# Another order for the weight pairs of a two-layer decoder step: a gate pair behind the pooling pair and one at the end, attention in ten pairs

## Chip, cores and metric

The kernel runs on one core of a Trainium2 chip. The time is the device time of one execution in microseconds; three runs of the kernel before took 1469.11 to 1471.54 us, with a median of 1469.99.

## What is computed

Two layers, each on 1024 prompt positions and 8 sample rows (T = 1032 columns). All columns of `w_in` come from one projection, then three branches are gated, projected and merged:

```python
xa, za, u, v, zb, q, k, vv, zc, gates = split_in(jnp.einsum('bld,de->ble', x, w_in))
ya = pool_mix(xa, 0, pos, pool_w, pool_scale)          # causal window sums of 2, 4, 8, 16, then a small matmul
yb = u * sgu_spatial(layer_norm(v), sgu_w, sgu_b)      # 128-position chunks
yc = banded_window_attention(rope(q), rope(k), vv, attn_sinks)
g = sigmoid(gates.reshape(lead + (3, D_MODEL)) + b_gate)
oa, ob, oc = (ya * silu(za)) @ w_pa, (yb * silu(zb)) @ w_pb, (yc * silu(zc)) @ w_pc
merged = g[..., 0, :] * oa + g[..., 1, :] * ob + g[..., 2, :] * oc
x = layer_norm(ALPHA * x + merged @ w_out, ln_g, ln_b)
```

## The kernel before

Every matrix product with fp32 data is made of three passes with a high and a low half of each operand (`split`, lines 97 and 98: ScalarE rounds to the high half, VectorE subtracts it from the original to get the low half). XH and XL hold the halves of x, transposed, for all 1032 columns.

The columns of `w_in` that don't need attention's rotary step are worked in 18 pairs of 128 columns each, from the weight `wS[l, p]`, p = 0 to 17: 12 gate pairs (p = 0 to 11, branch i = p // 4, columns d and d + 1), the pooling input xa (12), za (13), zb (14), u (15) and two pairs of zc (16, 17). A pair (`pair`, line 863) is a Strassen-like scheme of seven products, in the order 11, 2, 21, 3, 1, 4, 22; a product is 24 matmuls of 128 x 258 (line 862), four PSUM banks (`acc`) are in use, and VectorE's adds (line 878) and a ScalarE copy (line 888) empty a bank before it is used again. The result goes to two tiles `O`, and `use` finishes them: for a gate pair, tanh on ScalarE (line 928) and a store of both tiles to HBM (`gd`, line 930, issued by ScalarE); for za and zb, tanh and a product on VectorE (line 628); for zc, tanh and two products on VectorE for each of 8 pieces (lines 941 and 942), which also multiply the attention result in place. Weight halves come from `prep`: POOL makes sums of the weight quarters (lines 210 to 219), ScalarE and VectorE split them, SyncE loads the raw weights in the order that `order()` lists (line 92).

The tiles u4 to u11 are single buffers that many stages use in turn: gate pairs write u6/u7 or u8/u9 by turns, za goes to u8/u9, the pooling input to u6/u7, its running sums to u4/u5 and u10/u11.

All other work lies beside the pairs as jobs (`Jobs`). A pair calls `pump` 21 times, three times in each product; each call is a tick. In a tick at most one job with matrix work runs, and list 1, attention, runs one for every `pace` ticks (2.8). Attention is 80 jobs with matrix work (scores, transposes, products with v) and as many without (query halves, norms, key halves). Pooling sums (`pool_sums`) are POOL additions in list 3 and VectorE steps in list 2 (widening, line 795; mean, line 805), each some ticks behind the other; `queue_mix` queues six small matmuls (line 821, with line 823 on VectorE behind each). `need(key)` runs whatever is left of a list up to that job at once. Each engine works its queue in the order in which the program issues it.

In the main loop the order is: rotary columns, 12 gate pairs with attention beside them, the pooling pair, za with the pooling sums beside it, zb with the mix, u with the chunk products, zc 0, zc 2, and then `project`. During the last pair, zc 2, hooks split the pooling and chunk branches into halves (`split_y`, four times) and group 0 of the attention branch (`split_c`); groups 1, 3 and 2 are split in the first three steps of `project`.

`project` (line 980) has 24 steps (i, d): branch i into output columns d. A step has two halves of columns, q = 0 into `att` banks and q = 1 into `acc` banks, two banks each of four. Line 1000 multiplies by the gate, which SyncE has loaded back from HBM (`load_gate`, line 973) into u4 to u7; for i > 0 POOL adds it to the merged result (line 1002), and the next gate is loaded into the freed half. The first six steps are (0,0), (1,0), (0,1), (1,1), (2,0), (2,1); a step with i = 0 or 1 has 24 matmuls (line 995), one with i = 2 has 48 and needs the four attention groups.

Of the kernel before, what the change touches and what calls it, by code (L numbers as in the profile page):

```python
# [8 lines left out]
F32 = mybir.dt.float32  # L9
# [12 lines left out]
T = S + NS  # L22
DM = 1024
SEGS = ((0, 384), (384, 384), (768, 264))
ALPHA = 4.0 ** 0.25
EPS = 1e-5


# [73 lines left out]
def trunk_kernel(  # L102
# [44 lines left out]
    def t_u(s, shape, dt=F32, name="u"):  # L147

        return big.tile([128] + shape, dt, tag=s, name=f"{name}{s}")
# [22 lines left out]
    def order():  # L172
        for l in range(L):
            yield from [wA[l, :, k] for k in range(8)]
            yield from [wB[l, j, :, 4 * h:4 * h + 4] for j in range(5) for h in range(2)]
            yield from [wS[l, p, q] for p in range(18) for q in range(4)]
            yield from [wP[l, d, :, h * 512:h * 512 + 512] for h in range(2) for d in range(2)]
            for d in range(2, 8):
                yield from [wP[l, d, :, h * 512:h * 512 + 512] for h in range(2)]
                if d >= 4:  # L180
                    yield wO[l, 0, :, d - 4]
            yield from [wO[l, 0, :, k] for k in range(4, 8)]
            yield from [wO[l, 1, :, k] for k in range(8)]
# [154 lines left out]
    class Layer:  # L338
        def __init__(self, l):
            self.l, self.c, self.jobs = l, LC[l], Jobs()  # L340
            self.s, self.pt, self.res, self.rr, self.row, self.y = [{} for _ in range(6)]
            self.late, self.step, self.out = deque(), 0, []
            self.jobs.pace = 2.8
            self.kT = t_u("u10", [T], F32, "kT")
            self.v = t_u("u11", [NB, 128], F32, "v")
            self.vs = lay.tile([NS, 128], F32, name="vs")
# [4 lines left out]
        def a0_post(self, b, p):  # L351
# [7 lines left out]
            V.bn_aggr(mv[:n], st[:n])  # L359
            rstd_of(mv, n, EPS)  # L360
            vn = vn_dst[:n]
# [267 lines left out]

        def out_of(self, O, c, q, s):  # L630
            o = q * HT + s * 258
            return O[c][:, o:o + 258]

        def pair_xa(self):
            self.xa = O = [t_u(f"u{6 + j}", [T], F32, "xa") for j in range(2)]

# [283 lines left out]
            out(0, 1)  # L920
            pump()

        def gates(self, i, d, extra={}):
            O = [t_u(s, [T], F32, "g") for s in (("u8", "u9") if d % 4 else ("u6", "u7"))]

            def use(c, q, s, p):
                o = O[c][:, q * HT + s * 258:q * HT + s * 258 + 258]
                A.activation(o, p, AF.Tanh, bias=self.c["h"][:, i * 8 + d + c:i * 8 + d + c + 1], scale=0.5)  # L928
                if s and (c, q) in ((1, 0), (0, 1)):
                    A.dma_start(out=gd[i][d + c], in_=O[c])  # L930

            self.pair(use, O, extra)

        def gate_c(self, j, extra={}):
            O = [t_u(s, [T], F32, "z") for s in (("u6", "u7") if j else ("u4", "u5"))]

            def use(c, q, s, p):
                e = slice(q * HT + s * 258, q * HT + s * 258 + 258)
                t, o, y = t_w2()[:, 0:258], O[c][:, e], self.ycr[:, j + c, e]
                A.activation(t, p, AF.Tanh, scale=0.5)  # L940
                V.scalar_tensor_tensor(o, t, 1.0, p, op0=ALU.add, op1=ALU.mult)
                V.scalar_tensor_tensor(y, o, 0.5, y, op0=ALU.mult, op1=ALU.mult)

            self.pair(use, O, extra)

        def split_y(self, j, eng=None):
            h, lo = [t_u(f"x{4 + 2 * j + i}", [T], F32R, "yh") for i in range(2)]
# [32 lines left out]
        def project(self):  # L980
            for x, (i, d) in enumerate(self.steps):
# [5 lines left out]
                for q in range(2):  # L987
# [10 lines left out]
                    for s in range(2):  # L998
                        g = t[:, q * HT + s * 258:q * HT + s * 258 + 258]
# [9 lines left out]
                        self.late.append((self.step + 1, lambda d=d, q=q, m=m[:, e]: self.merged(d, q, m)))  # L1009
                    if (i < 2 and q) or (i == 2 and not q and d >= 3):  # L1010
                        prep()
                if x < 3:
                    self.split_c((1, 3, 2)[x])
                if x == 0:
                    for q in range(2):
                        self.load_gate(0, 1, q)
# [16 lines left out]
        def d_mm(self, b, h, w):  # L1033
# [10 lines left out]
            r = self.row[b][h]  # L1044
            V.scalar_tensor_tensor(r[:n], x[:n, 0:512], 2 * ALPHA, p[:n], op0=ALU.mult, op1=ALU.add)  # L1045
            V.bn_stats(self.rr[b][:n, h * 6:h * 6 + 6], r[:n])  # L1046

        def d_ln(self, b):
# [3 lines left out]
            V.bn_aggr(mv[:n], st[:n])  # L1052
            rstd_of(mv, n, 4 * EPS)
            g, be = c["lng"], c["lnb"]
# [82 lines left out]
    for l in range(L):  # L1137
        y = Layer(l)
        J = y.jobs
# [33 lines left out]
                J.need(("TT", n, k))  # L1173
        y.t1_parts()
        y.queue_sample()
        for i in range(3):
            for d in range(0, 8, 2):
                if (i, d) == (0, 2):
                    J.need("sp")
                y.gates(i, d, {3: lambda: J.need(("T1", 3))} if (i, d) == (0, 0) else {})  # L1180
        J.need(("P", NB - 1, 1))
        y.pair_xa()
        y.ya = y.pair_z(("u8", "u9"))
        y.queue_mix()
        J.need(("pool", 1))
# [3 lines left out]
        y.pair_u()  # L1189
        J.need(("sgu", 1))  # L1190
        y.gate_c(0)
        y.open_gates()
        for i, d in ((0, 0), (1, 0)):
            for q in range(2):
                y.load_gate(i, d, q)
        y.gate_c(2, {2: lambda: y.split_y(0), 21: lambda: y.split_y(1), 3: lambda: y.split_y(2),
                     1: lambda: y.split_y(3), 4: lambda: y.split_c(0)})
        for q in range(2):
            y.load_gate(1, 1, q)
        cur["w0"] = w0 = Slices(WA)  # L1200
# [8 lines left out]
        for i, (b, h) in enumerate(seq):  # L1209
# [9 lines left out]
            if h:  # L1219
                y.d_ln(b)  # L1220
                j = i - 9
# [119 lines left out]
```

## Time and profile before

| | us |
|---|---|
| median of three runs | 1469.99 |
| profiled execution, device time | 1468.98 |
| its span, first to last instruction | 1467.2 |
| TensorE matmuls busy in it | 1436.6 |
| VectorE busy | 1030.5 |
| ScalarE busy | 603.3 |
| POOL busy | 438.7 |

The granted TensorE clock is at its upper level throughout (mean 0.999). Times in the trace are counted from the start of the span. In the first layer the pairs run from 107.58 to 539.97 us and `project` begins at 539.97; the second layer repeats the pattern some 727 us later.

### The profile page before, as it was taken

How to read it: one execution, taken by the hardware profiler on the slowest of the kernel's cores; microseconds unless marked ns; L12 is line 12 of the kernel's file. 1: busy time of each engine (PE TensorE's matmuls, PEld its weight loads, DVE VectorE, ACT ScalarE, POOL GpSimd, SP SyncE). 2: the span in 40 equal slices, each digit the busy share in tenths (PEclk: the TensorE clock that was granted, in tenths of full speed). 3: DMA queues.
4: the chain of work that ended last, by engine and by line, in shares of the span. 5: the costliest groups of instructions: out<-in, count | busy, mean ns of one | idle time of the engine just before them, and what ended most of it. 6: DMA issues, size and time to landing. Idle time of an engine off the chain costs nothing. (4 is left out here: it accounts for less than half of the span.)

```text
span 1467.2 us, 27711 instructions
## 1 busy us (share of the span) xinstructions
PE 1436.6 (98%) x10592; PEld 1356.2 (92%) x10592; DVE 1030.5 (70%) x2330; ACT 603.3 (41%) x1419; POOL 438.7 (30%) x434
## 2 busy tenths in 40 slices
PE   7999999999999999999999999999999999999997
PEld 7999999999998999988799999999999999999876
DVE  6997676676558687654889966666665777966547
ACT  4375565556533252220224745555565232422100
POOL 0114334141242205500530251423321522054015
PEclk9999999999999999999999999999999999999999
DMA  6312222323223135643324122222222231466413
GB/s 253 125 46 80 87 94 66 102 73 102 73 84 76 44 102 188 204 142 94 134 93 139 53 73 96 79 95 73 86 89 102 55 83 38 132 187 194 130 48 126
DMA packets 82388, 151.92 MB, mean 104 GB/s; under 512 B 13216, under 2 KB 22512, under 8 KB 82224
## 3 DMA queue, kind: packets, MB, share of 16 engines
q1 hardware_dynamic: 65184, 114.34, 25.6%
q10 hardware_dynamic: 17072, 35.81, 6.3%
q8 instruction: 83, 1.36, 0.4%
q14 instruction: 49, 0.40, 0.1%
HBM read 113.62 MB, written 38.58 MB: 104 GB/s over the span
## 5 line engine op out<-in xcount | busy, mean ns | idle before, releaser
L862 PE MATMUL acc<-XH,wh 128*128 128x258 f32 x1152 | 235.9, 286 | 2.0 <-DVE zyu L878 2.0
L862 PE MATMUL acc<-XH,wl 128*128 128x258 f32 x1152 | 236.1, 286 | 0.0
L862 PE MATMUL acc<-XL,wh 128*128 128x258 f32 x1152 | 235.2, 285 | 0.0
L98 DVE TENSOR_TENSOR wl<-wr,wh 128x512 fp32r<-128x512 f32 x196 | 161.1, 822 | 97.3 <-ACT wh L97 96.7
L862 PEld LDWEIGHTS acc<-XH,wh 128*128 128x128 f32 x1152 | 178.7, 189 | 7.2 <-issue 6.5
L862 PEld LDWEIGHTS acc<-XH,wl 128*128 128x128 f32 x1152 | 178.4, 189 | 5.5 <-issue 5.0
L862 PEld LDWEIGHTS acc<-XL,wh 128*128 128x128 f32 x1152 | 178.7, 189 | 4.7 <-issue 4.2
L97 ACT ACTIVATE wh<-wr 128x512 fp32r<-128x512 f32 x196 | 122.3, 624 | 116.3 <-PE acc L862 48.2
L211 POOL TENSOR_TENSOR st<-st,wr 128x512 f32<-128x512 f32 x36 | 49.5, 1376 | 312.0 <-DVE wl L98 230.7
L98 DVE TENSOR_TENSOR wl<-st,wh 128x512 fp32r<-128x512 f32 x108 | 76.9, 712 | 71.9 <-ACT wh L97 71.1
L1002 POOL TENSOR_TENSOR glu<-glu,glu 128x516 f32<-128x516 f32 x56 | 80.8, 1460 | 145.9 <-DVE glu L1000 117.1
L319 PE MATMUL acc<-slx,XH 128*128 128x512 f32 (+1 forms) x384 | 114.1, 379 | 0.4 <-DVE slx L98 0.4
L878 DVE TENSOR_TENSOR gu<-gu,acc 128x258 f32<-128x258 f32 x240 | 89.7, 414 | 29.5 <-PE acc L862 29.5
L928 ACT ACTIVATE gu<-gu,halves 128x258 f32<-128x258 f32 x144 | 65.6, 504 | 104.7 <-DVE gu L878 104.2
L862 PE MATMUL acc<-T2x,wh 128*128 128x258 f32 x576 | 98.1, 287 | 1.2 <-DVE yc L395 1.2
L862 PE MATMUL acc<-T3x,wh 128*128 128x258 f32 x576 | 96.2, 286 | 1.6 <-DVE gu L878 1.6
L486 ACT ACTIVATE ap<-ap,ns 128x256 f32<-128x256 f32 (+1 forms) x128 | 62.4, 489 | 83.7 <-DVE ns L484 82.9
L862 PE MATMUL acc<-T4x,wh 128*128 128x258 f32 x576 | 96.1, 285 | 0.0
L210 POOL TENSOR_TENSOR st<-wr 128x512 f32<-128x512 f32 x36 | 50.7, 1407 | 143.2 <-DVE wl L98 66.5
L218 POOL TENSOR_TENSOR st<-wr,st 128x512 f32<-128x512 f32 x36 | 50.1, 1391 | 121.7 <-issue 121.3
L862 PEld LDWEIGHTS acc<-T2x,wh 128*128 128x128 f32 x576 | 80.9, 189 | 3.5 <-DVE yc L395 1.4
L319 PEld LDWEIGHTS acc<-slx,XH 128*128 128x128 f32 x384 | 71.9, 191 | 11.7 <-DVE slx L98 0.9
(246 smaller groups left out, 3444.8 us busy)
## 6 DMA issues: line engine op xcount, KB each, us to landing
wr<-in_wS_dram SPq DMA_DIRECT2D x144, 256.0 KB
gd<-gu ACTq DMA_DIRECT2D x48, 516.0 KB
glu<-gd SPq DMA_DIRECT2D x96, 258.0 KB
wr<-in_wP_dram SPq DMA_DIRECT2D x32, 256.0 KB
wr<-in_wO_dram SPq DMA_DIRECT2D x32, 256.0 KB
wr<-in_wB_dram SPq DMA_DIRECT2D x20, 256.0 KB
w<-in_xp_dram SPq DMA_DIRECT2D x16, 256.0 KB
w<-x2d SPq DMA_DIRECT2D x16, 256.0 KB
```

Of the source, the lines that this page charges most:

```text
L97: nc.scalar.activation(h, raw, AF.Copy)
L98: (eng or nc.vector).tensor_tensor(lo, raw, h.bitcast(F32), op=ALU.subtract)
L210: G.tensor_tensor(s1[:, 0:512], a21, a22, op=ALU.add)
L211: G.tensor_tensor(s2[:, 0:512], s1[:, 0:512], a11, op=ALU.subtract)
L218: G.tensor_tensor(s4[:, 0:512], a12, sums[p][1], op=ALU.subtract)
L319: PE.matmul(p[:, 0:n], x[:, k, blk(b)], c, start=(i == 0 and j == 0), stop=(i == len(terms) - 1 and j == len(t) - 1))
L486: A.activation(o, o, AF.Exp, bias=nm[:, i:i + 1], scale=-1.0, accum_out=su[:, i:i + 1])
L862: PE.matmul(ps[s][:, 0:258], a[:, c], b[:, s * 258:s * 258 + 258], start=(first and k == 0 and j == 0), stop=(k == 3 and j == 2), skip_gro ...
L878: V.tensor_tensor(part(c, q, s), part(*a, s), b[s][:, 0:258], op=ALU.add)
L928: A.activation(o, p, AF.Tanh, bias=self.c["h"][:, i * 8 + d + c:i * 8 + d + c + 1], scale=0.5)
L1002: (V if last else G).tensor_tensor(m[:, e], m[:, e], t[:, e], op=ALU.add)
```

## The change

The weight order becomes `PAIRS`: ten gate pairs, the pooling pair, gate pair 10 (branch 2, columns 4 and 5), za, zb, u, zc 0, zc 2, and gate pair 11 (branch 2, columns 6 and 7). Attention's pace goes from 2.8 to 2.3 ticks, and its end is asked for behind the tenth gate pair. Gate pair 10 writes u8/u9, which za takes next; zc 0 writes u6/u7 and zc 2 u4/u5 (before: u4/u5 and u6/u7); gate pair 11 writes u6/u7. The hooks with the branch splits now belong to gate pair 11, and attention's group 1 is split there too, behind group 0; `project` splits group 3 in its first step and group 2 in its second. The loads of gates (0,0) and (1,0) are issued ahead of the last pair and those of (1,1) behind it, as before.

```diff
+PAIRS = (0, 1, 2, 3, 4, 5, 6, 7, 8, 9, 12, 10, 13, 14, 15, 16, 17, 11)
@@ order()
-            yield from [wS[l, p, q] for p in range(18) for q in range(4)]
+            yield from [wS[l, p, q] for p in PAIRS for q in range(4)]
@@ Layer.__init__
-            self.jobs.pace = 2.8
+            self.jobs.pace = 2.3
@@ gates, gate_c
-        def gates(self, i, d, extra={}):
-            O = [t_u(s, [T], F32, "g") for s in (("u8", "u9") if d % 4 else ("u6", "u7"))]
+        def gates(self, i, d, us, extra={}):
+            O = [t_u(s, [T], F32, "g") for s in us]
-        def gate_c(self, j, extra={}):
-            O = [t_u(s, [T], F32, "z") for s in (("u6", "u7") if j else ("u4", "u5"))]
+        def gate_c(self, j):
+            O = [t_u(s, [T], F32, "z") for s in (("u4", "u5") if j else ("u6", "u7"))]
@@ project
-                if x < 3:
-                    self.split_c((1, 3, 2)[x])
+                if x < 2:
+                    self.split_c((3, 2)[x])
@@ main loop
-        for i in range(3):
-            for d in range(0, 8, 2):
-                if (i, d) == (0, 2):
-                    J.need("sp")
-                y.gates(i, d, {3: lambda: J.need(("T1", 3))} if (i, d) == (0, 0) else {})
+        for i, d in [(i, d) for i in range(3) for d in range(0, 8, 2)][:10]:
+            if (i, d) == (0, 2):
+                J.need("sp")
+            y.gates(i, d, ("u8", "u9") if d % 4 else ("u6", "u7"),
+                    {3: lambda: J.need(("T1", 3))} if (i, d) == (0, 0) else {})
         J.need(("P", NB - 1, 1))
         y.pair_xa()
+        y.gates(2, 4, ("u8", "u9"))
         y.ya = y.pair_z(("u8", "u9"))
         y.queue_mix()
         J.need(("pool", 1))
...
         y.gate_c(0)
+        y.gate_c(2)
         y.open_gates()
         for i, d in ((0, 0), (1, 0)):
             for q in range(2):
                 y.load_gate(i, d, q)
-        y.gate_c(2, {2: lambda: y.split_y(0), 21: lambda: y.split_y(1), 3: lambda: y.split_y(2),
-                     1: lambda: y.split_y(3), 4: lambda: y.split_c(0)})
+        y.gates(2, 6, ("u6", "u7"), {2: lambda: y.split_y(0), 21: lambda: y.split_y(1), 3: lambda: y.split_y(2),
+                                     1: lambda: y.split_y(3), 4: lambda: (y.split_c(0), y.split_c(1))})
```

## Rows read from the trace of the kernel before

A stretch in group 3 shows its bounds in us from the span's start, its length, the busy time and the instructions of PE, PEld, DVE, ACT and POOL, the granted clock, the DMA share and GB/s.

**Rows 1.** The page, part 1: busy us, share of the span, instructions.

```profile
PE 1436.6 (98%) x10592; PEld 1356.2 (92%) x10592; DVE 1030.5 (70%) x2330; ACT 603.3 (41%) x1419; POOL 438.7 (30%) x434
```

**Rows 2.** TensorE's waits, whole span: who waited for whom, total us, times, longest.

```profile
PE att L995 <- ACT ychx L97: 3.1, 2, 1.5
...
PE acc L862 <- DVE zyu L878: 2.0, 2, 1.0
...
PE att L821 <- DVE xau L805: 1.2, 2, 0.6
...
PE att L995 <- DVE yclu L98: 1.1, 2, 0.6
PE att L821 <- DVE zyu L823: 1.0, 2, 0.5
```

**Rows 3.** Stretches: nine attention pairs, xa, za, zb, six steps of project.

```profile
158.85:381.96 223.11, 223.11 (x1830) 214.00 (x1829) 148.53 (x418) 128.76 (x343) 68.37 (x76) 1.00 0.26 86
...
406.31:426.55 20.24, 20.24 (x170) 20.24 (x169) 9.44 (x18) 6.38 (x13) 3.84 (x3) 1.00 0.35 103
426.55:448.19 21.64, 20.65 (x170) 20.39 (x169) 19.05 (x27) 5.68 (x13) 17.55 (x15) 1.00 0.16 47
448.19:473.68 25.49, 24.37 (x183) 22.71 (x181) 20.64 (x48) 8.81 (x20) 5.71 (x5) 1.00 0.37 89
...
539.97:567.01 27.04, 24.46 (x194) 23.60 (x193) 21.81 (x42) 8.92 (x14) 9.18 (x7) 1.00 0.49 147
```

**Rows 4.** Timeline of VectorE in za: start, us, line, operation, count, idle before.

```profile
434.35 0.74 DVE L878 TENSOR_TENSOR zyu<-zyu,acc 128x258 f32<-128x258 f32 x2
...
436.25 0.74 DVE L628 SCALAR_TENSOR_TENSOR zyu<-w,acc 128x258 f32<-128x258 f32 x2
436.92 1.71 DVE L795 SCALAR_TENSOR_TENSOR pxyu<-pxyu,cb 128x512 f32<-128x512 f32 x1
...
444.52 0.74 DVE L878 TENSOR_TENSOR zyu<-zyu,acc 128x258 f32<-128x258 f32 x2
```

**Rows 5.** Timeline of POOL in the same stretch.

```profile
434.49 1.29 POOL L211 TENSOR_TENSOR st<-st,wr 128x512 f32<-128x512 f32 x1
435.73 2.34 POOL L775 TENSOR_TENSOR pxyu<-pxyu 128x1022 f32<-128x1022 f32 x1
```

**Rows 6.** Timeline of VectorE, first microseconds of zb.

```profile
453.79 1.39 DVE L805 SCALAR_TENSOR_TENSOR xau<-pxyu,cb,xau 128x496 f32<-128x496 f32 x2
```

**Rows 7.** Timelines of ScalarE, VectorE and TensorE, first steps of project.

```profile
543.79 0.76 ACT L940 ACTIVATE w<-zu 128x258 f32<-128x258 f32 x2 [2.09 <-DVE zu L878]
...
544.97 1.05 ACT L97 ACTIVATE ychx<-yc 128x1032 fp32r<-128x1032 f32 x1
...
545.50 0.43 DVE L942 SCALAR_TENSOR_TENSOR yc<-zu,yc 128x258 f32<-128x258 f32 x1
545.85 0.75 DVE L1000 SCALAR_TENSOR_TENSOR glu<-glu,att 128x258 f32<-128x258 f32 x2
...
547.78 1.23 DVE L98 TENSOR_TENSOR yclu<-yc,ychx 128x1032 fp32r<-128x1032 f32 x1
...
551.52 2.32 DVE L98 TENSOR_TENSOR yclu<-yc,ychx 128x1032 fp32r<-128x1032 f32 x1
553.76 0.74 DVE L1000 SCALAR_TENSOR_TENSOR glu<-glu,att 128x258 f32<-128x258 f32 x2
...
554.32 0.63 PE L995 MATMUL att<-ychx,wh 128*128 128x258 f32 x2 [1.53 <-ACT ychx L97]
```

**Rows 8.** Timeline of VectorE and TensorE at the start of the fourth gate pair.

```profile
184.85 0.69 DVE L98 TENSOR_TENSOR wl<-wr,wh 128x512 fp32r<-128x512 f32 x1 [1.18 <-ACT wh L97]
...
185.98 0.92 PE L862 MATMUL acc<-T2x,wh 128*128 128x258 f32 x4
...
186.97 0.64 PE L862 MATMUL acc<-T2x,wh 128*128 128x258 f32 x4
```

**Rows 9.** DMA queue of ScalarE, 408.0 to 410.6: packets, MB, share; store issued at 408.02.

```profile
q10 hardware_dynamic: 143, 0.53, 50.8%
```

More of the change, by code (lines that the diff above doesn't have):

```diff
@@ L942, in use @@
                 V.scalar_tensor_tensor(y, o, 0.5, y, op0=ALU.mult, op1=ALU.mult)
-            self.pair(use, O, extra)
+            self.pair(use, O)
         def split_y(self, j, eng=None):
```

## The prediction, made before the change was run

> **What bounds the kernel now.** I read the busy shares first: TensorE works in 98% of the span, VectorE in 70% [rows 1]. The change neither adds nor removes a matrix instruction: the same 18 pairs with 168 matmuls each, the same attention, pooling and gate work, in another order. So the time can only move by what TensorE waits, and the second view is the list of its waits [rows 2]. Those that lie where the change works are, over both layers: 3.1 and 1.1 us for the halves of the attention branch (`split_c`), 1.2 and 1.0 us for the pooling results (line 805) and the mix (line 823), 2.0 us for an add of line 878 in a z pair. Together 8.4 us. The third view says where they fall [rows 3]: the pooling pair, which has no attention, takes 20.24 us, which is the plain price of a pair (168 matmuls, 0.1205 us each); the pair behind it (za) takes 21.64, so 1.4 are lost; the next (zb, with the six mix steps) 25.49, of which 1.1 are waits by [rows 2] (half of 1.2 and 1.0). The first six steps of `project`, 192 matmuls, would take 192 x 0.1205 = 23.1 us and take 27.04: 3.9 lost. Per layer that is 6.4 us around the change. The nine attention pairs from the third on have no idle time in the table: 223.11 of 223.11 us.
>
> **Pooling sums.** By the ticks of `Jobs` (21 in a pair), the pooling steps end 31 ticks behind the pooling pair: half 0's at tick 18 (sum at 2, then 3, 4, 4, 4 and 1 ticks on), and half 1's, queued behind them, need 4 each for the second widening and the two means and 1 for the sample. Before, za has 21, and `need(("pool", 1))` throws what is left (one widening, two means, the sample) into VectorE's queue at the start of zb: the double mean of 1.39 us at 453.79 [rows 6] is what the fourth mix step waits for, and the mix behind it (line 823) is late in turn. After the change the gate pair and za give 42 ticks; the rest falls in za's first ten, ten ticks ahead of the first mix. Both waits go: 1.1 us a layer, with the slow restart behind each 1.2. What would be late next there is the z products of za, and VectorE has room: 19.05 busy us in za before, of which the sums' first part moves away.
>
> The other loss, 1.4 us in za, I let move along into the new gate pair. Its cause stands in VectorE's rows [rows 4]: the add at 444.52 ends a queue without a pause, in which the widening at 436.92 took 1.71 us, although a mean of the same size takes 0.7 [rows 6], and ended 0.6 us behind the POOL addition that ran from 435.73 for 2.34 us [rows 5]. A line 878 add, which reads PSUM, took its usual 0.74 for two under the POOL addition at 434.49. So SBUF-to-SBUF work on VectorE sits out POOL's additions, and those follow the pooling pair wherever it stands. A gate pair lacks the z products (line 628: 0.74 us for two), but the one ahead of that add, at 436.25, ended before the stretched widening and lay inside POOL's addition anyway. I take 0 as the gain, with 0 and 1.4 as the ends.
>
> The Trainium skill ("SBUF — State Buffer", "SBUF: two separate sides") says that VectorE and GpSimd share one port pair as an exclusive lock, and that a VectorE operation with two SBUF inputs blocks for the whole of a GpSimd operation that reads SBUF; these rows agree. By it the move alone buys nothing at this add; without it I would have counted 1.2 us more a layer, 2.4 in all.
>
> The new gate pair writes u8 and u9, and za writes them next, so za waits for the stores. A store of 516 KB has 143 of its 144 packets through within 2.6 us of its issue [rows 9]. The later one is issued some 3 us into za, and its tile is first written 5.8 us into za: hidden, with TensorE needing the bank only at 8.7. If VectorE runs 2 us later still, it costs up to 1 us; I take 0.
>
> **The last pair and the first steps of `project`.** Out of the last pair go 16 z products of 0.43 us on VectorE, 6.9 us; in come one more attention split of 1.23 us on VectorE and as much on ScalarE, and no product (tanh is ScalarE's alone) [rows 7]. The pair keeps TensorE's plain 20.24 us, with its end at 539.97 [rows 3]. The matter is when VectorE gets to line 1000: now 5.9 us behind the end of the pair (545.85 against 539.97), and to the third step's product 13.8 us behind it (553.76). TensorE's fifth step starts at 554.32 and needs both that product (it frees the two PSUM banks) and the split of group 2; the list names the split, but the product ended within 0.2 us of it. So an earlier split alone would free nothing. After the change the way to the first product is not VectorE's amount but a chain through both engines: add, tanh, two splits, add, tanh. Product 1 ends 5.8 us ahead of the pair's end. An add (0.75), two tanh (0.8 to 0.9), a chunk split (1.05 on ScalarE, 1.23 on VectorE), a weight half (0.6) and the next add (0.75) end 0.8 ahead of it; two tanh and the store's issue (1.0), two splits on ScalarE (2.1), the second on VectorE (1.3), a weight half (0.6) and the last add (0.75) end 4.8 behind it [rows 4, 7, 8], instead of 5.9; from there to the third step's product lie, as before, two splits, one of them stretched by POOL (2.32 against 1.23), so 7.9 to 8.5 us: 12.7 to 13.4; I take 13.3. The fifth step then starts 0.5 us earlier, and the wait for the second half of group 2 (0.6, with the restart 0.9) is gone, as this split now stands ahead of that product. Gain 1.4 us a layer; ends 0 (chain as late as now) and 3.4 (chain as early as VectorE's amount allows).
>
> Gate loads: line 973 for (1, 1) now waits on SyncE for the last gate store into u6, and the loads of (0, 1) and two weight loads queue behind it. Store out at about 5.4 us behind the pair, landed at 8 [rows 9], both loads issued by 9.5 and in by 12, against 13.3 when VectorE comes to them: hidden by 1.3 us. If that cover is gone, it costs what it is short, up to 1.5 us a layer.
>
> **Attention in ten pairs.** 80 matrix jobs at a pace of 2.3 ticks are 184 ticks; from the start in the first pair they end in the tenth, so nothing is forced. A pair's attention grows by 2.8/2.3: VectorE now spends 148.53/9 = 16.5 us a pair, 9.4 of them without attention [rows 3], so 7.1 become 8.6; TensorE's 4.55 become 5.5. VectorE's share goes from 67% to 70%: not a bound. But it is the queue that counts: a weight half that waits 1.18 us for ScalarE, held up by the exponentials, stands ahead of an add, and the four matmuls that need the bank take 0.92 us instead of 0.64 [rows 8]: 0.28 us, and it comes back in every second pair up to the twelfth, too short for the list of waits. The pattern shifts to another phase: such a meeting comes up less often by the ticks (scores right behind product 4 twice instead of five times), yet scores and their norm stand two ticks apart instead of three. I take 0.4 us a layer as a cost; ends -0.7 and +4.
>
> **Sum.** Per layer -1.2 - 1.4 + 0.4 = -2.2; two layers -4.4. The profiled execution took 1468.98 us, of which 1467.2 are span and 1.8 lie around it; 1468.98 - 4.4 = 1464.6. The median of the runs is 1.0 above it: 1465.6.
>
> **Rivals.** (a) VectorE's chain into `project` comes no earlier: the fifth step waits for the product alone, and only the pooling wait goes: 2 x (1.2 - 0.4) = 1.6, so 1468.4. For it: the product ended together with the split; against: 6.9 us of work leave. Chance 0.20. (b) Everything goes: 1.2 + 1.2 + 3.4 a layer and no cost in attention, 11.6: 1458.4. For it: three of the four causes are queues on VectorE, which loses work in each pair concerned; against: POOL's additions. 0.14. (c) Slower: denser attention makes scores, norm and weight halves meet in most pairs; a wait of 0.5 us in each of 9 pairs is 9 us in two layers; with the gain of 5.2 that stays, 1473.8. It eats the gain at 5.2 / 18 = 0.29 us a pair and is told as slower from (5.2 + 2.9) / 18 = 0.45. For it: 0.28 us in every second pair now; against: the ticks. 0.11. (d) The gate store holds the first loads by 1.5 us a layer: 1468.6. 0.05. My forecast has 0.50, with 1463 to 1468 as its own range.
>
> **How the numbers follow.** A measurement of this kernel tells 0.2%, 2.9 us, from no change: faster is below 1467.05. That takes 0.47 of my own case and (b): 0.61; within 0.2% are (a), (d) and the rest: 0.28; slower (c): 0.11. The range leaves out the lower part of (b) and (c): 1459.5 to 1471.
>
> **What would show it.** In the changed kernel's waits the rows for lines 805 and 823 are gone; the wait of about 1 us for line 878 stands in the gate pair behind the pooling pair; za takes 20.3 and zb 24.3 us. The first six steps of `project` take about 25.6 us, and the wait ahead of (2, 0) is put down to line 1000. The ten attention pairs stay free of waits over 0.3 us, apart from the first two. Wrong would be: project's start at 27 us (a) or at 23.6 (b), attention pairs with waits of 0.5 us (c), or a wait of line 1000 for a DMA (d).

## The result, and the profile after

The changed kernel took 1510.57 us (median of 5 runs, 1509.82 to 1516.33), beside 1471.54 us for the kernel before on the same chip (1469.11 to 1472.21). The ratio is 1.0279, with a 95% interval of 1.0268 to 1.0291: 41 us slower, where I had forecast 4 us faster. The profiled execution has a span of 1508.8 us; before it was 1467.2. Lines of the changed kernel are those of before plus one: a product is line 863, an add 879, ScalarE's copy out of PSUM 889, the tanh 929, a matmul of `project` 996, a gate product 1001.

Part 1 of the page answers [rows 1]: the same 10592 matmuls, 20 us more in TensorE's busy time, and 22 us more in VectorE's.

```profile
PE 1456.7 (97%) x10592; PEld 1367.8 (91%) x10592; DVE 1052.8 (70%) x2330; ACT 600.2 (40%) x1419; POOL 437.6 (29%) x434
```

A matmul's record is longer where the granted clock is lower or its start is held (four matmuls of a product take 0.64 us, 1.06 at 222.80 us at half the clock, 0.96 behind the wait at 219.69), so "busy" grows with the trouble and doesn't explain it. TensorE's waits answer [rows 2] (who waited for whom, total us, times, longest):

```profile
PE acc L863 <- DVE gu L879: 13.7, 16, 1.8
...
PE att L996 <- DVE glu L1001: 7.4, 2, 4.8
PE acc L863 <- ACT gu L889: 3.5, 6, 1.3
PE att L509 <- DVE ap L499: 3.2, 6, 0.7
...
PE acc L863 <- DVE zyu L879: 1.9, 1, 1.9
```

The rows for the pooling result and the mix (lines 805 and 823 before) are gone, as predicted. In their place a product waits 13.7 us for VectorE's add in a gate pair, where before had only this:

```profile
PE acc L862 <- DVE gu L878: 1.6, 2, 0.8
```

The waits for a gate product in `project` come to 7.4 us (1.0 before), and two rows are new: a product for ScalarE's copy (3.5) and attention's transposes for the norm (3.2). The stretches show where (bounds in us, length, busy time of PE, PEld, DVE, ACT, POOL, granted clock, DMA share, GB/s): the ten attention pairs of layer 0, the last eight of them, the pooling pair, the new gate pair, za, zb, and the first six steps of `project` in layers 0 and 1. They answer [rows 3].

```profile
107.78:381.82 274.04, 263.34 (x2087) 246.62 (x2085) 190.47 (x513) 151.66 (x416) 88.21 (x107) 0.99 0.23 76
159.74:381.82 222.08, 213.21 (x1685) 198.45 (x1683) 152.02 (x417) 123.79 (x340) 62.10 (x72) 0.99 0.23 76
381.82:402.06 20.24, 20.24 (x171) 20.24 (x169) 9.44 (x18) 6.44 (x13) 3.85 (x3) 1.00 0.33 102
402.06:423.76 21.70, 20.71 (x170) 20.38 (x169) 18.19 (x23) 5.98 (x13) 17.45 (x15) 1.00 0.18 48
423.76:447.89 24.13, 22.37 (x169) 22.03 (x169) 17.72 (x38) 9.16 (x20) 5.85 (x5) 0.93 0.35 94
447.89:471.59 23.70, 23.70 (x182) 22.51 (x181) 15.70 (x31) 7.45 (x17) 5.12 (x4) 1.00 0.26 90
558.28:585.54 27.26, 24.35 (x195) 23.58 (x194) 19.11 (x35) 9.05 (x13) 9.40 (x7) 1.00 0.54 182
1303.34:1335.29 31.95, 26.81 (x195) 26.12 (x194) 19.09 (x35) 9.06 (x13) 9.37 (x7) 0.89 0.45 156
```

**The balance.** From the third gate pair to the pooling pair, before took 406.31 - 158.85 = 247.46 us for ten pairs [rows 3]; less two plain pairs of 20.24 that is 206.98 for the same attention in eight, and now it is 222.08: 15.1 us more. With the first two pairs it is 15.8 (258.25 to 274.04) in layer 0, and 16.3 in layer 1: 32 of the 41.6 us by which the span grew. Za is 2.5 us longer (21.64 to 24.13) in layer 0 and 3.3 in layer 1, although its old loss of 1.4 us now stands in the new gate pair (21.70 against 20.24); zb is 1.8 shorter in each; the first six steps of `project` are 0.2 and 4.9 us longer. With the 1.5 us in each new gate pair these make 42.4; 0.8 goes the other way elsewhere.

**One stall in attention.** Timelines of ScalarE, VectorE and TensorE in layer 0 (start, us, line, operation, idle before it). Attention's score matmuls had been put right behind product 4.

```profile
214.13 0.91 ACT L929 ACTIVATE gu<-gu,halves 128x258 f32<-128x258 f32 x2 [2.70 <-DVE gu L879]
...
215.45 0.42 ACT L456 ACTIVATE ksu<-yc 64x256 fp32r<-64x256 f32 x1 [0.40 <-ACT gu L929]
216.87 0.51 ACT L487 ACTIVATE ap<-ap,ns 128x256 f32<-128x256 f32 x1 [1.01 <-DVE ns L485]
...
217.97 0.61 ACT L98 ACTIVATE wh<-wr 128x512 fp32r<-128x512 f32 x1
...
215.90 0.42 DVE L457 SCALAR_TENSOR_TENSOR ksu<-yc,ksu 64x256 fp32r<-64x256 f32 x1 [1.46 <-ACT ksu L456]
216.35 0.48 DVE L485 CUSTOM_DVE_ANT_0 ap<-att,cb,skn 128x256 f32<-128x256 f32 x1
...
218.61 0.69 DVE L99 TENSOR_TENSOR wl<-wr,wh 128x512 fp32r<-128x512 f32 x1 [1.18 <-ACT wh L98]
219.22 0.75 DVE L879 TENSOR_TENSOR gu<-gu,acc 128x258 f32<-128x258 f32 x2
...
219.69 0.96 PE L863 MATMUL acc<-T2x,wh 128*128 128x258 f32 x4 [1.72 <-DVE gu L879]
```

Read it from the end: the product waited 1.72 us for an add, and the add stood in VectorE's queue behind a weight half (line 99). That half waited for its other half on ScalarE (line 98), which stood behind two exponentials (line 487), which waited for VectorE's score reductions (line 485), which came behind the query copies (456, 457) that ScalarE could only begin when the tanh before them was done. Each engine was idle for a part of this; no engine is short of time. It is one chain that goes from ScalarE to VectorE, back, and to VectorE again, and its end comes late enough to hold up the add.

### The profile page after: what moved, and what is told of

The parts are those of the page before. It is cut to its first block, busy times and chain, and to the rows that moved or that the text cites. A ratio compares the mean times of both kernels' runs of the same rounds, so it can differ in the third digit from the quotient of the medians.

```text
span 1508.8 us, 27697 instructions
## 1 busy us (share of the span) xinstructions
PE 1456.7 (97%) x10592; PEld 1367.8 (91%) x10592; DVE 1052.8 (70%) x2330; ACT 600.2 (40%) x1419; POOL 437.6 (29%) x434
## 4 chain that ended last, share of the span: by engine, by line
PE 60%; DVE 21%; ACT 9%; issue 6%; DMA 1%; POOL 1%; ACTq 1%; SPq 0%; DVEq 0%; POOLq 0%
PE acc L863 30%; PE acc L320 12%; PE att L996 6%; PE acc L996 5%; DVE wl L99 5%; ACT gu L929 3%; ACT wh L98 2%; ACT ap L487 2%; PE acc L621 2%; DVE ap L499 2%; DVE gu L879 2%; DVE ap L485 1%; DVE ksu L457 1%; PE att L520 1%; PE att L479 1%
## 5 line engine op out<-in xcount | busy, mean ns | idle before, releaser
L863 PE MATMUL acc<-XH,wh 128*128 128x258 f32 x1152 | 239.6, 288 | 8.7 <-DVE gu L879 4.4
L99 DVE TENSOR_TENSOR wl<-wr,wh 128x512 fp32r<-128x512 f32 x196 | 156.1, 797 | 95.9 <-ACT wh L98 95.3
L863 PEld LDWEIGHTS acc<-XH,wh 128*128 128x128 f32 x1152 | 179.8, 189 | 15.8 <-ACT gu L889 4.8
L863 PE MATMUL acc<-T2x,wh 128*128 128x258 f32 x576 | 101.8, 296 | 9.2 <-DVE gu L879 7.8
L863 PEld LDWEIGHTS acc<-T3x,wh 128*128 128x128 f32 x576 | 81.9, 192 | 6.8 <-DVE gu L879 2.1
```

Of the source, the lines that this page charges most:

```text
L99: (eng or nc.vector).tensor_tensor(lo, raw, h.bitcast(F32), op=ALU.subtract)
L863: PE.matmul(ps[s][:, 0:258], a[:, c], b[:, s * 258:s * 258 + 258], start=(first and k == 0 and j == 0), stop=(k == 3 and j == 2), skip_gro ...
```

## The experiments

The theories: **density** (ten pairs hold more attention each, so the small queues overflow), **phase** (what counts is in which product of a pair a score job falls; before had a harmless pattern, fifteen jobs in two pairs, that came back every two pairs), **order** (the new sequence of pairs itself). Where no interval is given, a time is that of one run, beside one of the kernel before on the same chip.

**Pace alone.** The kernel before, with one number changed:

```diff
-            self.jobs.pace = 2.8
+            self.jobs.pace = 2.3
```

> The kernel before with attention's pace at 2.3 ticks instead of 2.8, nothing else: attention is done in ten of the twelve gate pairs, the last two are plain. Theory A (attention in ten pairs is what costs; the changed kernel's ten attention pairs took 274 us a layer where the share of the twelve was 258): the time rises by 2 x 16 = 32 us, to about 1502, and the same kinds of waits show (line 878, 888 and 498 ahead of TensorE, 0.3 to 1.7 us each, in pairs 3 to 10). Rival B (the order of the pairs and their tiles or weights is what slows the ten pairs): the time stays within 4 us of before.

It took 1501.59 us (before: 1472.63). Its ten attention pairs are those of the changed kernel, in layer 0 eight of them to within 0.05 us (27.05, 24.88, 26.44, 27.94 against 27.07, 24.89, 26.45, 27.97 for the first four), and the two gate pairs behind them are plain, 20.24 each. So 29 us come from one number, without any new order.

**A pace between.** Pace 2.75: only 2% denser than before.

> The kernel before with pace 2.75 instead of 2.8. The density of attention is 2% higher, but the jobs no longer fall on the same ticks of every second pair. If density is the cause of the loss, the cost is a tenth of that of 2.3, about 3 us or less: 1471 to 1473. If it is the phase (2.8 is 15 jobs in 42 ticks, so one pattern, which happens to be harmless, repeats), each pair meets other patterns and the cost is near that of 2.3: 1485 to 1502.

1498.49 us, nearly as slow. TensorE's waits:

```profile
PE acc L862 <- DVE gu L878: 9.0, 10, 2.3
...
PE acc L862 <- ACT gu L888: 7.1, 11, 1.3
```

Before, the first row is 1.6 us, and the second isn't there. A cost that does not shrink with the density is not a cost of density: at 2.75 the jobs drift through the pair instead of coming back to the same ticks.

**The same density, shifted.** The kernel before with its pace of 2.8, the first of these jobs held back:

```diff
             self.jobs.pace = 2.8
+            self.jobs.free = 120.8
```

> The kernel before, its order of pairs and its pace of 2.8 ticks between attention's matrix jobs unchanged; only the first of these jobs of each layer starts 23.8 ticks later, so that all of them fall at other ticks of the gate pairs (the score jobs now behind product 2 or 3 of some pairs and in product 22 of others). Density theory (a stall comes from more attention work in a pair): the work in each pair is as before, so the time is that of before, 1472 us within 3. Phase theory (a stall comes from where in a pair a score job falls): pairs with a wait of 0.6 us or more of a product for VectorE's add or ScalarE's copy appear, and the time is 1482 to 1502 us, as in the run with a pace of 2.75.

1490.83 us (before: 1469.42), inside what phase said. And it holds its own control: the two layers begin attention at different ticks, and layer 0 pays nearly all: its first twelve pairs are 19.1 us longer than before, those of layer 1 2.2. Two pairs with the same jobs in layer 0 and in layer 1:

```profile
209.19:263.32 54.13, 52.15 (x408) 48.37 (x409) 36.46 (x96) 29.25 (x79) 14.63 (x17) 1.00 0.24 79
951.46:1001.82 50.36, 50.03 (x411) 47.73 (x409) 33.59 (x94) 29.30 (x79) 14.32 (x16) 1.00 0.25 84
```

3.8 us for two pairs, at the same work and the same granted clock.

**Fixed ticks, at the highest density.** If phase is all, ten jobs a pair at well chosen ticks should cost nothing, although that is a third more a pair than before. I let the matrix jobs run only at listed ticks of each pair:

```diff
+SLOTS = (0, 2, 5, 7, 8, 9, 11, 14, 16, 18)
...
-                if i == 1 and self.tick < self.free:
+                if i == 1 and not self.allowed():
```

Here `allowed` asks whether the tick within the pair is in the list. First in the order of before:

> The kernel before, its order of pairs unchanged, but attention done in ten pairs, its matrix jobs at fixed ticks of each pair that put the four score jobs of a pair in product 11, at the end of product 3, in product 21 and in product 4. Density theory: ten pairs at ten per cent or more of further work stall as in the run with a pace of 2.3, near 1500 us. Phase theory: the pairs of attention have no wait over 0.3 us of a product, take some 26 us each in every pair alike, and the time is that of before, 1472 us within 4.

1512.87 us: a miss. Attention's transposes now came ahead of the norm that they need; TensorE's longest row is this one:

```profile
PE att L516 <- DVE ap L506: 18.2, 21, 2.8
```

Taken alone the run fits density as well as a badly chosen list. Then the changed kernel with the same list, and with the two repairs that are told further down:

> The changed kernel with three things undone at once: the stores of the pooled sums issued by SyncE, the loads of the gates of step (0,1) issued right behind the last pair, and attention's matrix jobs at the same fixed ticks as in the run of before with fixed ticks. Phase theory: attention falls from 274 to some 259 us a layer (32 us of both layers' cost), the pooling pair to 21.3 us, the project's first six steps to 26.2 us; the time is 1466 to 1473 us. Density theory: attention stays near 274 us a layer and the time is near 1500 us.

1508.14 us, for the same reason. And with every second tick, (0, 2, 4 to 18):

> As the run before it, but with the matrix jobs at every second tick of a pair, so that the score jobs fall at products 11, 21, 1 and 4. Density theory: near 1500 us, the same as with the other fixed ticks. Phase theory: the time hangs on the ticks alone; score jobs behind product 1 cost nothing or up to 1 us a pair, so 1466 to 1485 us, and differs from the other fixed ticks by what the waits of the products at those ticks add up to.

1490.38 us, and this one decides. The list goes by a count of ticks that stands four higher at the first pair of layer 0 than at that of layer 1, so the same list gives the layers different places. The fifth pair of each layer, with the same sixteen score, sixteen transpose and sixteen value matmuls:

```profile
209.24:236.28 27.04, 27.04 (x219) 25.22 (x217) 19.52 (x58) 16.50 (x47) 8.94 (x12) 1.00 0.23 78
944.64:973.76 29.12, 27.78 (x217) 25.35 (x217) 20.83 (x58) 16.27 (x49) 8.99 (x12) 1.00 0.23 74
```

In layer 0 TensorE has no idle time in six such pairs running, denser than any pair of the changed kernel. Density is not the cause.

**The good places in both layers.** I counted the ticks from the first pair of each layer, so that both should have the places of that layer 0, with one tick changed in each layer to see more. In the order of before, and in the new order with both repairs:

> The kernel before, its order of pairs unchanged, attention in ten pairs with the matrix jobs at the ticks that fell out in the first layer of the run with every second tick (score jobs in product 2 behind its second third, at the end of products 21 and 1, and in product 22), counted from the first pair of each layer so that both layers have them; the two layers differ in one or two ticks. Phase theory: no wait of a product over 0.3 us in the pairs of attention in either layer, twelve gate pairs of 299 to 304 us, the time 1470 to 1480 us. Density theory: near 1500 us, since each pair carries a third more of attention than in before.

> The changed kernel with the stores of the pooled sums on SyncE, the loads of the gates of step (0,1) right behind the last pair, and the same ticks as the run beside it. Phase theory: attention as in the run beside it, and the new order of pairs is worth what its other parts measured with their two disturbances gone, 0.7 us at the pooling pairs and 0.7 us at the project in each layer, so 2 to 3 us below that run: 1467 to 1477 us. If the order costs something that no run has shown yet, the time is above that of the run beside it.

1495.45 and 1490.13 us: both missed, since the first score job came one place late and every later job moved on by one. Even so the prediction of "no wait over 0.3 us" held in layer 1, by luck of the place, while layer 0 had transposes waiting 1.03 and 0.5 us in each pair. With the first job put right:

> As the run of the changed kernel before it, whose first job of each layer came one place late, so that every later job fell one tick place on; here the first score job is back at the start of the second pair, and the four score jobs of a pair fall in product 2, at the end of products 21 and 1, and in product 22. The layers differ in one tick each: the first does the value products in product 11 one tick later, the second the transposes ahead of them one tick earlier. Phase theory: no wait of a product or a transpose over 0.3 us in the ten pairs, 26.4 to 27.0 us for each of the middle ones, 296 to 303 us for the twelve gate pairs of a layer, the time 1460 to 1470 us. Density theory: near 1490 us again.

> The kernel before, its order of pairs unchanged, with attention in ten pairs at the same ticks as the run beside it. Phase theory: 1463 to 1473 us, 2 to 3 us above the run beside it, which is what the order of pairs is worth with its disturbances gone. If the order itself costs time, this run is the faster of the two.

1480.38 and 1482.77 us (before: 1472.21), above the 1460 to 1470 and the 1463 to 1473 said. Between the two lie 2.4 us, where 2 to 3 were said, but each is one run. Layer 0 is as wanted (27.0 us a pair, waits of 0.13 at most in the middle pairs). Layer 1, which differs in one transpose a tick earlier and one value product a tick earlier, pays 0.9 us or more for an add in each pair from the fourth on. So my rule for choosing ticks isn't good enough, but what the ticks do is plain. The time of the first twelve pairs of a layer, by run (in the new order these hold the pooling pair and the new gate pair, 1.5 us more):

| kernel | matrix jobs a pair | layer 0, us | layer 1, us |
|---|---|---|---|
| before | 7.5 | 298.7 | 297.1 |
| shifted (`b_shift2`) | 7.5 | 317.8 | 299.3 |
| pace 2.75 (`b_pace275`) | 7.6 | 313.1 | 312.3 |
| pace 2.3 (`b_pace23`) | 9.1 | 313.2 | 314.3 |
| changed kernel | 9.1 | 316.0 | 314.9 |
| `b_slota` | 10 | 313.2 | 326.3 |
| `a_slota` | 10 | 313.6 | 327.4 |
| `a_slotb` | 10 | 303.3 | 319.5 |
| `b_good` | 10 | 320.7 | 300.1 |
| `a_good` | 10 | 322.3 | 299.9 |
| `b_good2` | 10 | 301.9 | 307.2 |
| `a_good2` | 10 | 303.4 | 309.8 |

At one density the sum goes from 300 to 327 us; at the density of before from 297 to 318. Where the waits are gone, packing ten jobs into a pair costs 1 to 3 us a layer against before (layer 0 of `a_slotb` and the two `good2` runs, layer 1 of the two `good` runs, less the 1.5 in the new order): that is what density is worth.

**The store of the pooled sums.** In za of the changed kernel (queue of ScalarE, VectorE and TensorE, layer 0; then layer 1):

```profile
424.60 0.33 ACTq L931 DMA_DIRECT2D gd<-gu  x1
424.97 1.91 ACTq L816 DMA_DIRECT2D out_dram<-ap  x1
...
427.64 0.69 DVE L99 TENSOR_TENSOR wl<-wr,wh 128x512 fp32r<-128x512 f32 x1 [2.42 <-ACT wh L98]
...
428.81 0.82 PE L863 MATMUL acc<-T2x,wh 128*128 128x258 f32 x2 [1.76 <-DVE gu L879]
...
1179.12 0.76 DVE L879 TENSOR_TENSOR zyu<-zyu,acc 128x258 f32<-128x258 f32 x2 [1.68 <-DMA gd<-gu]
...
1179.60 1.35 PE L863 MATMUL acc<-T3x,wh 128*128 128x258 f32 x4 [1.87 <-DVE zyu L879]
```

The new place of the pooling puts its small store (line 816: 60 KB, 1024 packets of 60 bytes) right behind a gate store on ScalarE's queue. In layer 0 its issue takes 1.91 us there and holds up a weight half. In layer 1 za's write into u8 waits for the gate store out of u8: issued at 1172.41, it has no packet on the queue before 1174.2 and its last by 1178.5, 6.1 us, where a store before took 2.6 [rows 9]. The small store's own packets were through by 1172.0, so they did not stand ahead of it; why it was late is open. One edit, the changed kernel otherwise:

```diff
-            A.dma_start(out=sps_o[l, :, j], in_=self.st[:, j, :, 1:16])
+            SP.dma_start(out=sps_o[l, :, j], in_=self.st[:, j, :, 1:16])
```

> The changed kernel with the store of the sample rows of the pooling state (line 816, 1040 small packets a layer half) issued by SyncE instead of ScalarE. In the changed kernel it stands on ScalarE right behind a gate store, at the start of za: its issue took 1.91 us there in the first layer, and the following gate store into which za's tile waits took 4.1 and 5.4 us. Theory: za's wait of 1.8 us (line 879) and the half clock behind it go, za falls from 24.1 and 25.0 to 20.3 to 21 us: 7 to 8 us less, about 1503. Rival (the tiles u8 and u9 are what za waits for, whatever the small store does): za stays at 23 or more.

1506.55 us, and za in the two layers:

```profile
424.96:446.24 21.28, 21.12 (x170) 20.60 (x170) 17.90 (x38) 9.04 (x20) 5.83 (x5) 1.00 0.34 104
1168.84:1190.08 21.24, 21.13 (x169) 20.61 (x169) 17.86 (x37) 9.05 (x20) 5.85 (x5) 1.00 0.34 104
```

2.9 and 3.7 us are gone there, and the half clock with them. The 1503 us said was missed: the first pair and the start of `project` in layer 0 are 1.5 and 2.0 us longer than in the changed kernel, each with a stretch at the lower clock (at 130.37 and 574.10) that the changed kernel doesn't have there. The Trainium skill ("DMA: Bandwidth & Descriptors", "Queues, rings and completion order") says that ScalarE and SyncE have a ring each on the same 16 engines, which take turns between rings by packets. No run here shows that turn-taking. SyncE issued the small store at 421.20, 4.6 us ahead of the gate store (425.79), and all its packets were through by 424.2. So the edit moved the store in time as well as to another queue, and which of the two counts was not tried.

**The gate loads of step (0, 1).** In `project` of the changed kernel (SyncE's queue, VectorE, TensorE):

```profile
566.82 0.81 SPq L974 DMA_DIRECT2D glu<-gd  x2
...
568.22 0.84 SPq L974 DMA_DIRECT2D glu<-gd  x2
...
572.96 0.76 DVE L1001 SCALAR_TENSOR_TENSOR glu<-glu,att 128x258 f32<-128x258 f32 x2 [0.93 <-issue]
...
1313.62 0.80 SPq L974 DMA_DIRECT2D glu<-gd  x2
...
1315.01 1.31 SPq L974 DMA_DIRECT2D glu<-gd  x3
...
1320.25 0.76 DVE L1001 SCALAR_TENSOR_TENSOR glu<-glu,att 128x258 f32<-128x258 f32 x2 [3.17 <-issue]
...
1320.82 0.82 PE L996 MATMUL att<-ychx,wh 128*128 128x258 f32 x2 [4.81 <-DVE glu L1001]
```

`project` begins at 558.12 and 1303.18 (its two windows above start 0.16 later). The loads of (1, 1) wait on SyncE for the store of the last gate out of u6, and those of (0, 1) queue behind them. They go out 10.1 us behind the pair (568.22) in layer 0 and from 11.8 on (1315.01) in layer 1, where the load that waits for the store goes out 4.7 us behind the store's issue (2.9 in layer 0); the product that needs them starts 14.8 and 17.1 us behind the pair. The edit issues them ahead of the loads that wait:

```diff
+        for q in range(2):
+            y.load_gate(0, 1, q)
         for q in range(2):
             y.load_gate(1, 1, q)
...
-                if x == 0:
-                    for q in range(2):
-                        self.load_gate(0, 1, q)
```

> The changed kernel with the gate loads of (0,1) issued behind the last pair and ahead of those of (1,1), instead of inside the first step of project. They go to u7, whose gate store is out 5.8 us earlier than that of u6. Theory (the product of step (0,1) waits for its load, which SyncE holds behind the wait for u6): VectorE's idle 0.9 and 3.2 us ahead of that product go, project's first six steps take 25.5 to 26.5 us instead of 27.3 and 32: 5 to 6 us less, about 1505. Rival (the loads are slow because the queues are full): no change beyond 1 us.

1505.79 us. The first six steps take 26.17 and 26.18 us in the two layers (27.26 and 31.95 in the changed kernel, 27.04 and 27.06 before), the product starts 13.8 behind the pair in both, and TensorE's wait there is 1.55 us.

**The order alone.** No run so far had the new order with attention as before. The attention of twelve pairs fits if the pooling pair and the gate pair behind it carry its end:

```diff
-            self.jobs.pace = 2.3
+            self.jobs.pace = 2.8
...
-        J.need(("P", NB - 1, 1))
         y.pair_xa()
         y.gates(2, 4, ("u8", "u9"))
+        J.need(("P", NB - 1, 1))
```

The pooling's history goes into a buffer of its own for this, for which two small buffers were cut.

> The changed kernel's order of pairs, with attention left as it was before the change: pace 2.8, over twelve pairs, which are now the ten gate pairs, the x pair of the pooling and the new gate pair behind it, so that the point at which attention must be done lies behind that gate pair. The history of the pooling is loaded into a buffer of its own. So this is the new order without the denser attention. My account of the changed kernel gives 32 of its 41 us to attention and 9 to the order with its two disturbances (the store of the pooled sums behind the gate store, the late loads of the gates of step (0,1)): 1476 to 1482 us. If the order itself is what costs, the time stays above 1495 us. If attention collides with the x pair or the pooling sums, waits appear in the eleventh or twelfth pair alone.

1477.74 us against 1469.57: ratio 1.0053, 95% interval 1.0038 to 1.0068. So the new order with its two disturbances, without denser attention, costs 8.2 us, inside what was said; `project` is 2.0 and 4.9 us longer in it than before, and za takes 23.01 and 23.32. The account by pairs had said 9. With the two repairs:

> As the run beside it, with the two disturbances gone as well: the stores of the pooled sums issued by SyncE, the loads of the gates of step (0,1) right behind the last pair. By the account the order is then worth 0.7 us at the pooling pairs and 0.7 us at the project in each layer, so 2 to 3 us under before: 1466 to 1469 us. If the order costs something that no run has shown, it is at or above before.

1467.99 us, ratio 0.9985 (0.9976 to 0.9995): as said, and the only version here below before. The last two attention pairs (the first is the pooling pair, the second the gate pair behind it), za, zb and the start of `project`, layer 0:

```profile
358.27:382.81 24.54, 24.54 (x206) 23.87 (x205) 14.92 (x48) 13.20 (x35) 4.20 (x3) 1.00 0.24 78
382.81:407.83 25.02, 24.77 (x199) 22.88 (x198) 20.01 (x41) 10.15 (x23) 14.40 (x14) 1.00 0.09 33
407.83:429.99 22.16, 20.68 (x170) 20.32 (x169) 19.12 (x34) 8.24 (x18) 7.42 (x6) 1.00 0.50 114
429.99:453.69 23.70, 23.70 (x182) 22.50 (x181) 16.08 (x32) 7.45 (x17) 5.12 (x4) 1.00 0.29 90
540.37:566.53 26.16, 24.29 (x195) 23.53 (x194) 18.99 (x35) 9.05 (x13) 9.43 (x7) 1.00 0.58 192
```

Five pairs of before (24.54, 24.35, 20.24, 21.64, 25.49) and a plain one, 136.50, are now these four and two plain ones, 135.90: 0.6 us; `project` gives 0.9. That is 1.5 us a layer, 3.0 in all, and the ratio says 2.2, with 0.7 to 3.5 as its ends.

## Why the prediction was wrong

**Attention in ten pairs: the step that failed.** I took 0.4 us a layer with ends of -0.7 and +4; it measured 15.8 and 16.3. I had found the mechanism (a weight half that waits for ScalarE behind the exponentials, ahead of an add [rows 8]) and named the phase, but I priced the new phase with the cost of the old one: 0.28 us, the meeting that was left in a pattern in which meetings happened to be short. Where the upper end of +4 came from, the prediction does not say. In the other places one meeting costs up to 1.72 us, and there are two kinds more, of which the list before has no row: the copy of line 889 behind the exponentials (1.3 us) and transposes that wait for the norm (0.7). Rival (c) had the sign and the place, and a price of 0.5 us a pair; it was 1.6. Its ground, denser attention, was wrong too: the pace of 2.75 costs almost as much as 2.3.

The waits over 0.06 us that the trace names for TensorE in layer 0's ten attention pairs grew by 8.7 us (2.0 to 10.7) of those 15.8. The half clock at 220.85 adds 1.5: the same pair, with a wait of 1.73 us in the same place and the clock at its upper level, took 27.62 in `b_pace23` against 29.11. The other 5.6 are in no list: slow restarts (0.96 us for four matmuls at 219.69, where [rows 8] has 0.64 without a wait) and the price of packing itself, 1 to 3 us by the runs with fixed ticks. This split is worked out, not measured.

VectorE's share came to 68% (152.02 of 222.08 us): not a bound, as said, and beside the point.

**Pooling sums: right.** The waits of lines 805 and 823 are gone, and zb is 23.70 in both layers: 1.8 us a layer, where I had said 1.2 (24.3). The loss in za moved into the new gate pair as I took it: TensorE waits 0.99 us there for the add of line 879, the pair costs 1.46 more than a plain one. VectorE and POOL there, in the changed kernel:

```profile
411.75 2.37 DVE L796 SCALAR_TENSOR_TENSOR pxyu<-pxyu,cb 128x512 f32<-128x512 f32 x1
...
414.65 0.74 DVE L879 TENSOR_TENSOR gu<-gu,acc 128x258 f32<-128x258 f32 x2
...
411.24 2.34 POOL L776 TENSOR_TENSOR pxyu<-pxyu 128x1022 f32<-128x1022 f32 x1
...
414.26 2.22 POOL L776 TENSOR_TENSOR pxyu<-pxyu 128x1020 f32<-128x1020 f32 x1
```

The widening takes 2.37 us and ends 0.5 behind the POOL addition that it began under; the two adds that read PSUM take their 0.74 under the next one. The rule of the Trainium skill ("SBUF — State Buffer", "SBUF: two separate sides") that a VectorE operation with two SBUF inputs contends with a GpSimd operation that reads SBUF gave this zero gain, and these rows agree. But za was to be 20.3; with its store repaired it is 21.3: 1.0 us stays there as one wait of 0.16 and slow starts, too short for the list.

**What the move put next to it: missed.** I asked what the gate store costs za (0, with up to 1 us if VectorE is late) and measured its length alone [rows 9]. I had not put the pooling's own DMA, line 816, into the step that moved it, nor asked what it would stand next to on ScalarE's queue. Its place there cost 2.9 and 3.7 us; in layer 1 it was even the u8 hazard that I had bounded by 1, at 1.87 us, for a reason not in the bound.

**The last pair and `project`.** The chain through ScalarE and VectorE was well sized: the first gate product starts 5.0 us behind the pair (4.8 said, 5.9 before). With the loads in time the third step's product starts at 13.8, no earlier than before (13.3 said): between the two VectorE waits 0.35 and 0.26 us for ScalarE's halves, and from product to product it takes 8.7 us, where I said 7.9 to 8.5. So the 0.5 us that I gave to an earlier fifth step did not come, as in rival (a); the 0.9 for the second half of group 2 did. The six steps take 26.16 (25.6 said): a gain of 0.9 us a layer where I said 1.4.

**Gate loads: rival (d), larger than its bound.** I had the loads issued by 9.5 and landed by 12. They were issued at 10.1 and from 11.8 on, with the product at 14.8 and 17.1: from the issue to the product 4.7 and 5.2 us passed, not the 2.6 of a lone store [rows 9]. SyncE had issued three other loads in the 1.4 us before, and the DMA engines were nearly full:

```profile
568.22:572.96 4.74, 2.73 (x23) 2.52 (x21) 3.81 (x4) 0.63 (x1) 2.72 (x2) 1.00 0.93 312
1315.01:1320.25 5.24, 1.00 (x9) 0.79 (x7) 2.07 (x1) 0.63 (x1) 0.98 (x1) 0.97 0.92 308
```

Layer 0 lost 1.1 us to it (27.26 against 26.17) and layer 1 5.8, where I had said up to 1.5 at a chance of 0.05. "Hidden by 1.3 us" was a margin taken from a quiet stretch for a busy one.

Without attention the sum was -5.2 us. Measured: +8.2 with the two DMA disturbances, -1.6 without them. The direction of each move was right; what each brought to stand beside it was not in the sum.

## What to carry to other kernels

Where several engines hand work round within a few microseconds, a pattern that runs without waits can owe it to its phase more than to its load, as here: before changing a pace, lay out the ticks of the new pattern, and bound the cost of a meeting by the whole chain (here tanh, copies, reductions, exponentials, weight half, add), not by the meetings that the present pattern happens to have. A pace whose pattern does not come back after one or two pairs, like 2.75 here, meets places that the old pattern never showed. When a step moves, list its DMAs and look at which store or load each will stand next to; count the loads ahead of one on its queue, and take its landing time from a stretch that is as busy as the new one.

## What the runs showed of the hardware

The granted clock fell to its lower level (1.2 of 2.4 GHz) inside the kernel, which before never did until its end. Two of five stretches:

```profile
220.85:224.25 3.40, 3.40 (x18) 3.40 (x17) 2.44 (x7) 2.60 (x6) 0.16 (x1) 0.50 0.77 287
...
1319.90:1326.70 6.80, 5.88 (x27) 5.91 (x28) 3.36 (x9) 0.00 (x0) 2.52 (x2) 0.50 0.46 158
```

The first begins 1.2 us behind the end of a wait of 1.72 us, the second lies on the end of a wait of 4.81 us. All five begin behind or within a wait of 1.7 us or more. Not every such wait brings one: layer 0 of `b_pace23` and of `a_swap` has the same wait of 1.73 us in the same pair, stays at the upper level and takes 27.62 and 27.63 us for the pair, against 29.11, so the lower clock cost 1.5 us; and before waits 2.75 us up to 10.20, with the granted clock at 1.00 from 4.9 to 20. Nor is such a wait needed: in `a_sps` the clock fell at 130.37, behind sixteen small matmuls of line 601 that took 1.95 us, with no wait over 0.06 us since 112.11. So what brings it on is not settled here. `b_shift2`, with no wait over 1.2 us in its gate pairs, has no such stretch until its end.

The store of 1024 small packets (60 KB) took 1.91 us to issue on ScalarE right behind the issue of a store of 516 KB in layer 0, and 0.45 us in the same place in layer 1 (1.60 and 1.90 in `a_late0`); the larger store's issue takes 0.33. What makes the difference was not tried.
